# 32 of 384 expert-layer tokens take their input products by gathered rows on GpSimd and ScalarE

## The chip, the cores and the metric

The kernel runs on one core of a Trainium2 chip. The metric is the device time of one execution in microseconds, and the time of a kernel is the median of its runs. The engines are called PE (TensorE, matmuls), DVE (VectorE), ACT (ScalarE), POOL (GpSimd) and SP (SyncE, which only issues DMAs). Times inside an execution are counted from the start of the profiled span.

## The reference, cut to what matters

The program is one transformer layer on 512 tokens of 1024 features: modulated normalisation, a mixer (windowed attention and a gated delta rule), a second normalisation, and then the expert layer. The change is nearly all in the expert layer. It has 16384 experts with one neuron each; every token picks 16 experts in each of 8 heads, so 128 (expert, gate) pairs:

```
def one_block(xt):                                   # 128 tokens x 1024
    q = (xt @ w_query).reshape(PEER_BLOCK, PEER_HEADS, 2, PEER_KEY_HALF)
    s = jnp.einsum('phxd,xkd->phxk', q, sub_keys)    # 128 keys in each half
    s_top, i_top = lax.top_k(s, PEER_TOPK)
    cand = (s_top[:, :, 0, :, None] + s_top[:, :, 1, None, :]).reshape(...)
    best, pos = lax.top_k(cand, PEER_TOPK)
    ...
    expert = i1 * PEER_N_KEYS + i2
    gate = jax.nn.softmax(best, axis=-1)
    act = jax.nn.gelu(jnp.einsum('phkd,pd->phk', u_tab[expert], xt))
    return jnp.einsum('phk,phkd->pd', gate * act, v_tab[expert])
```

The output is sum over the chosen experts of gate times gelu(u_e . x) times v_e. u_tab and v_tab have 16384 rows of 1024 f32 values, 64 MB each.

## The kernel before

The 512 tokens are four tiles of 128, which stand in four *slots*. The SLOT table says which tile stands in which slot.

**Slots 0 to 2 (384 tokens) are dense.** All 16384 experts are computed for them, as 128 groups "e" of 128 experts. For each e, SP loads the 512 KB of the input table (peer_ut) and of the output table (peer_v). ACT and DVE split each load into two f16 parts (t_usplit: ACT L2056, DVE L2058; t_vsplit: ACT L2131, DVE L2133), so that three f16 matmuls stand for one f32 matmul. t_u makes the U product, 24 matmuls of 384 columns per e (8 slices of the features by 3 passes); t_act applies the gelu on ACT and keeps the result (a buffer of `acts`, or a *spill* to DRAM). t_g multiplies it by the gates (DVE L2147), splits it (ACT L2152, DVE L2154), and t_v makes the V product, 18 matmuls of 512 columns per e (3 slots, 2 halves of the features, 3 passes), which add up in six banks over all 128 e. So a V product needs the gates of all 384 tokens, while a U product needs none.

**The gates** are made dense as follows. For each slot the product-key scores are taken (t_q, t_score), and DVE finds the top 16 (t_top, t_slot: MAX8, FIND_INDEX8 and MATCH_REPLACE8 instructions, then a number of small ones; L1925 is the last). Then t_gates makes 8 chunks of 16 tokens per slot: four one-hot instructions of 128x2048 f16 on DVE (L1980, L1982, L1984, L1986), 128 small matmuls that scatter the gates to 128x128 per token, four ACT copies, and a 1 MB write to DRAM (wd). When all 24 chunks are written, the event ev_wall is set, and t_wread, t_vload and t_v start. The wd of eight e at a time is read back in one transfer.

**Slot 3 (128 tokens) is the gather slot.** POOL issues one indirect DMA of 128 rows (512 KB) for each of the 128 choices, first from peer_u, then from peer_v (t_gather, L2224; four row buffers). DVE makes a dot product with each row of peer_u (L2234) and an accumulation with each row of peer_v (L2256).

**The order of instructions.** Every `t_...` function is a task that yields the cost of its next step before issuing it. A planner (Driver) keeps a clock for each engine, and always issues the waiting step of the best priority among those that could start within a small window. Each engine's instruction order in the program is therefore fixed ahead of the run. The dictionary X holds priorities and window sizes. During the run an engine works through its list in that order, and waits where its next instruction isn't ready.

At the program's start ada_group (called by t_ada1) loads the eight 1 MB blocks of the first third of w_ada, and PE multiplies them by the conditioning vector; all else waits for that modulation.

## Time and profile before

| what | value |
|---|---|
| median of 3 runs | 1710.05 us (1708.99 to 1712.87) |
| the profiled execution, its own time | 1712.26 us |
| its span | 1710.5 us |
| PE busy | 1609.8 us, 94% of the span |
| DVE busy | 1444.0 us, 84% |
| ACT busy | 791.0 us, 46% |
| POOL busy | 478.1 us, 28% |
| moved by DMA | 405.16 MB, mean 237 GB/s |
| the chain of work that ended last | PE 39%, DVE 20%, DMA 10% of the span |

Busy shares are means over stages with different limits. The span is best read in three stretches: up to about 635 us the mixer and the queries (the first slot's scoring ends there), from there to about 861 us the scoring and the one-hots, with U products on PE beside them, and from 861 us, where the first V matmul starts, the U and V products with the gathers. The profiled execution's time is 1.8 us over its span.

### The profile page before, as it was taken

How to read it: one execution, taken by the hardware profiler on the slowest of the kernel's cores; microseconds unless marked ns; L12 is line 12 of the kernel's file. 1: busy time of each engine (PE TensorE's matmuls, PEld its weight loads, DVE VectorE, ACT ScalarE, POOL GpSimd, SP SyncE). 2: the span in 40 equal slices, each digit the busy share in tenths (PEclk: the TensorE clock that was granted, in tenths of full speed). 3: DMA queues.
4: the chain of work that ended last, by engine and by line, in shares of the span. 5: the costliest groups of instructions: out<-in, count | busy, mean ns of one | idle time of the engine just before them, and what ended most of it. 6: DMA issues, size and time to landing. Idle time of an engine off the chain costs nothing.

```text
span 1710.5 us, 29276 instructions
## 1 busy us (share of the span) xinstructions
PE 1609.8 (94%) x11075; PEld 978.2 (57%) x11075; DVE 1444.0 (84%) x2884; ACT 791.0 (46%) x1386; POOL 478.1 (28%) x351
## 2 busy tenths in 40 slices
PE   3999998988896999999999999999999999899997
PEld 1665557887655885677655555555555554444443
DVE  3678658988989999999988888888888888798887
ACT  2665658766533434566543333333333333244441
POOL 0200332323001000000014445445466556554300
PEclk9999999999998999999999999999999999999999
DMA  9335442211333303699969999999999999888762
GB/s 378 113 128 187 155 179 81 70 56 45 109 112 134 114 2 124 191 272 279 325 241 354 348 369 344 374 364 350 347 377 330 367 363 331 315 317 331 270 244 86
DMA packets 157727, 405.16 MB, mean 237 GB/s; under 512 B 12681, under 2 KB 71561, under 8 KB 152465
## 3 DMA queue, kind: packets, MB, share of 16 engines
q1 hardware_dynamic: 120720, 269.06, 45.1%
q0 software_dynamic: 36864, 134.23, 21.4%
q8 instruction: 86, 1.41, 0.3%
q14 instruction: 57, 0.46, 0.1%
HBM read 366.59 MB, written 36.65 MB: 236 GB/s over the span
## 4 chain that ended last, share of the span: by engine, by line
PE 39%; DVE 20%; DMA 10%; issue 5%; POOL 2%; ACT 1%; POOLq 0%; DVEq 0%; ACTq 0%; SPq 0%
PE bank L207 38%; DMA arena<-in_peer_v,arena 8%; DVE arena L2058 3%; POOL arena L2224 2%; DVE arena L1986 1%; DVE arena L1984 1%; DVE arena L1980 1%; DVE arena L1982 1%; DVE arena L2256 1%; DMA arena<-in_peer_u,arena 1%; DVE arena L1816 1%; DVE arena L1818 1%; DVE arena L1822 1%; DVE arena L1814 1%; DVE arena L1759 1%
## 5 line engine op out<-in xcount | busy, mean ns | idle before, releaser
L207 PE MATMUL bank<-arena 128*128 128x384 f16 (+9 forms) x10610 | 1566.5, 316 | 49.4 <-DVE arena L1105 6.8
L207 PEld LDWEIGHTS <-arena 128*128 128x128 f16 (+1 forms) x9528 | 826.9, 98 | 626.8 <-issue 46.1
L2224 POOL DMA_INDIRECT arena<-in_peer_u,arena x128 | 161.1, 1258 | 515.2 <-DMA arena<-in_peer_ut 339.0
L2224 POOL DMA_INDIRECT arena<-in_peer_v,arena x128 | 211.8, 1655 | 160.6 <-DVE arena L2256 140.4
L2056 ACT ACTIVATE arena<-arena 128x1024 f16<-128x1024 f32 x128 | 135.1, 1056 | 253.9 <-PE bank L207 184.5
L2131 ACT ACTIVATE arena<-arena 128x1024 f16<-128x1024 f32 x128 | 134.2, 1050 | 136.4 <-PE bank L207 101.0
L2256 DVE SCALAR_TENSOR_TENSOR arena<-arena 128x1024 f32<-128x1024 f32 x126 | 160.2, 1280 | 36.9 <-DMA arena<-in_peer_v,arena 36.7
L2133 DVE TENSOR_TENSOR arena<-arena 128x1024 f16<-128x1024 f32 x128 | 156.0, 1219 | 29.2 <-ACT arena L2131 29.0
L2058 DVE SCALAR_TENSOR_TENSOR arena<-arena 128x1024 f16<-128x1024 f32 x128 | 155.9, 1220 | 26.5 <-ACT arena L2056 26.3
L2234 DVE SCALAR_TENSOR_TENSOR arena<-arena 128x1024 bf16<-128x1024 f32 x128 | 156.3, 1221 | 23.6 <-DMA arena<-in_peer_u,arena 22.8
L2152 ACT ACTIVATE arena<-arena 128x384 f16<-128x384 f32 x128 | 66.4, 519 | 170.6 <-DVE arena L2147 170.4
L207 PEld LDWEIGHTS bank<-arena 128*128 128x128 f32 (+1 forms) x1082 | 114.5, 178 | 36.0 <-DMA arena<-in_w_ada 12.3
L2154 DVE TENSOR_TENSOR arena<-arena 128x384 f16<-128x384 f32 x128 | 70.6, 552 | 6.6 <-ACT arena L2152 6.6
L1063 POOL TENSOR_TENSOR arena<-arena 128x512 f32<-128x512 f32 x12 | 17.9, 1495 | 203.7 <-DVE arena L1060 203.7
L2147 DVE TENSOR_TENSOR arena<-arena 128x384 f32<-128x384 f32 x128 | 70.5, 551 | 1.5 <-DMA arena<-wd 1.5
L1998 ACT ACTIVATE arena<-bank 128x512 f32<-128x512 f32 x96 | 51.7, 598 | 24.9 <-PE bank L207 17.8
L1105 DVE TENSOR_TENSOR arena<-bank,arena 128x512 f16<-128x512 f32 x72 | 49.0, 685 | 15.9 <-PE bank L207 11.5
L2091 ACT ACTIVATE arena<-bank 128x384 f32<-128x384 f32 x128 | 60.7, 475 | 1.6 <-DVE arena L2154 1.2
L1113 ACT ACTIVATE arena<-bank 128x512 f16<-128x512 f32 x60 | 35.8, 597 | 22.4 <-PE bank L207 21.3
L810 DVE SCALAR_TENSOR_TENSOR arena<-arena 128x770 f32<-128x770 f32 (+1 forms) x48 | 44.1, 928 | 0.8
L1529 POOL TENSOR_TENSOR arena<-arena 128x1024 f32<-128x1024 f32 x4 | 9.4, 2348 | 116.5 <-DVE arena L1527 104.0
L1118 ACT ACTIVATE arena<-bank 128x512 f16<-128x512 f32 x60 | 35.5, 596 | 6.2 <-PE bank L207 4.5
(256 smaller groups left out, 1275.0 us busy)
## 6 DMA issues: line engine op xcount, KB each, us to landing
arena<-in_peer_ut SPq DMA_DIRECT2D x128, 512.0 KB, 5.8
arena<-in_peer_v SPq DMA_DIRECT2D x128, 512.0 KB, 6.4
arena<-in_w_ada SPq DMA_DIRECT2D x24, 1024.0 KB, 8.7
wd<-arena SPq DMA_DIRECT2D x24, 1024.0 KB, 6.9
arena<-wd SPq DMA_DIRECT2D x16, 1536.0 KB, 10.3
arena<-in_w_int SPq DMA_DIRECT2D x21, 512.0 KB, 4.4
arena<-in_wq SPq DMA_DIRECT2D x16, 512.0 KB, 3.6
arena<-in_x SPq DMA_DIRECT2D x8, 512.0 KB, 4.6
```

Source lines behind the costliest of these rows:

```text
L207: PE.matmul(out, lhsT=l, rhs=r, start=start, stop=stop, skip_group_check=True)
L2056: A.activation(hl[0], Ud[e], AF.Copy, scale=US)
L2058: V.scalar_tensor_tensor(hl[1], Ud[e], US, hl[0], op0=OP.mult, op1=OP.subtract)
L2091: A.activation(Aw[e], b[:, 0:ND], AF.Gelu, scale=1.0 / US)
L2131: A.activation(hl[0], Vd[e], AF.Copy)
L2133: V.tensor_tensor(hl[1], Vd[e], hl[0], op=OP.subtract)
L2147: V.tensor_tensor(a3, a3, Wr[w][:, :, e % 8], op=OP.mult)
L2152: A.activation(g[0], a, AF.Copy)
L2154: V.tensor_tensor(g[1], a, g[0], op=OP.subtract)
L2224: G.indirect_dma_start(out=r, out_offset=None, in_=io[name], in_offset=bass.IndirectOffsetOnAxis(ap=gidx[:, p:p + 1], axis=0))
L2234: V.scalar_tensor_tensor(scr, r, 1.0, h2g, op0=OP.mult, op1=OP.mult, accum_out=gact[:, p:p + 1])
L2256: V.scalar_tensor_tensor(y, r, gact[:, p:p + 1], y, op0=OP.mult, op1=OP.add)
```

## The change

Thirty-two of the 384 dense tokens, the last 32 of slot 2 (HT = 32, HS = 2), are taken out of the U product, which becomes 352 columns wide (NU). Their activations come from gathered rows, by a new task t_hyb with its helper t_hu: when slot 2's scoring is done, DVE computes the expert numbers (L2240 in the new file), eight DMAs spread them and the 32 tokens' features over 128 partitions (4 choices of a token stand side by side), POOL gathers 32 times 128 rows of peer_u (L2251) into three row buffers, POOL multiplies each by the features (L2259, 128x1024 f32), ACT sums each product along the row (L2261), and at the end come one gelu, four small DMAs back and a DVE product with the gates (L2276). Only then do slot 2's one-hots start (t_gates waits for ev_hyb), and the main gather too. For these 32 columns the dense gate matrix holds gate times activation already, so t_g copies them on ACT rather than multiplying (one more ACT instruction per e), and DVE multiplies 352 columns instead of 384. The V product is as wide as before.

Slot 2, of which the 32 tokens are, is now scored first, then slot 3 and the other two; SLOT puts other tiles in the slots. The three V buffers (vst) are the row buffers of the 32 gathers, handed over after the last of them. ada_group issues its loads before it waits for the conditioning vector. fetch and some other steps tell the planner of extra waiting times ("wait", numbers in X), the limit of spills is 40 instead of 20 (24 are used, before 5), and the numbers in X are other ones.

```diff
-    SLOT = {1: 0, 2: 1, 0: 2, 3: 3}
+    SLOT = {1: 2, 2: 3, 0: 0, 3: 1}
@@ ada_group
         for k in range(KT):
             yield ("spawn", load(k), prio + 0.01 * k)
+        ps = yield get(bank)
+        yield ready
@@ t_ada1
-        b = yield get(pj)
-        yield ev_c0
-        yield from ada_group(0, ada_first, 1, b)
+        b = yield from ada_group(0, ada_first, 1, pj, ev_c0)
@@ _peer
+    HT, HS = 32, 2
+    NU, HQ = ND - HT, 128 // HT
-    vst = Res([reg(101 + 4 * i, [D]) for i in range(3)])
+    vst = Res([])
@@ t_q
+            yield put(hrow, *[reg(kb, [D]) for kb in (57, 61, 65)])
@@ t_gates
+        if s == HS:
+            yield ev_hyb
@@ t_u
-                        mm(b[:, 0:ND], Uw[e][j][:, k], h2hl[i][:, k, 0:ND], k == 0 and n == 0, k == KT - 1 and n == 2)
+                        mm(b[:, 0:NU], Uw[e][j][:, k], h2hl[i][:, k, 0:NU], k == 0 and n == 0, k == KT - 1 and n == 2)
@@ t_g
-            yield dv(ND)
-            V.tensor_tensor(a3, a3, Wr[w][:, :, e % 8], op=OP.mult)
+            yield later(ac(HT, 0, 1))
+            A.activation(a3[:, NCU:], Wr[w][:, NCU:, e % 8], AF.Copy)
+            yield dv(NU)
+            V.tensor_tensor(a3[:, 0:NCU], a3[:, 0:NCU], Wr[w][:, 0:NCU, e % 8], op=OP.mult)
@@ new
+    def t_hyb():
+        yield ev_pair[HS]
+        yield ev_mem1
+        up = slice(128 - HT, 128)
+        i1, i2, g = [pairs[HS]["ii"][up, x].rearrange("p k h -> p (k h)") for x in range(3)]
+        yield dv(128)
+        V.scalar_tensor_tensor(hstage[up], i1, 128.0, i2, op0=OP.mult, op1=OP.add)
+        t = TILE[HS]
+        for q in range(HQ):
+            yield later(dm(HT * 256))
+            sync.dma_start(hidx[q * HT:(q + 1) * HT], hstage[up, q * HT:(q + 1) * HT])
+            yield later(dm(HT * 4096))
+            sync.dma_start(h2g[q * HT:(q + 1) * HT], h2d[(t + 1) * 128 - HT:(t + 1) * 128, :])
+        yield ("join",)
+        for n in range(HT):
+            r = yield get(hrow)
+            yield ("POOL", 1.45)
+            G.indirect_dma_start(out=r, out_offset=None, in_=io["peer_u"],
+                                 in_offset=bass.IndirectOffsetOnAxis(ap=hidx[:, n:n + 1], axis=0))
+            yield ("spawn", t_hu(n, r, g, up), X['pht'])
+    def t_hu(n, r, g, up):
+        yield dm(128 * 4096)
+        yield ("wait", X["whu"])
+        yield ("POOL", 2.9)
+        G.tensor_tensor(r, r, h2g, op=OP.mult)
+        yield ("wait", X["wpa"])
+        yield ac(1100, 0, 1)
+        A.activation(scr, r, AF.Copy, accum_out=hact[:, n:n + 1])
+        yield put(hrow, r)
...
+        yield put(vst, *(yield get(hrow, 3)))
+        yield ac(HT, 0, 1)
+        A.activation(hact, hact, AF.Gelu)
+        for q in range(HQ):
+            yield later(dm(HT * 256))
+            sync.dma_start(hmove[up, q * HT:(q + 1) * HT], hact[q * HT:(q + 1) * HT])
+        yield ("join",)
+        yield ("wait", 5.0)
+        yield dv(128)
+        V.tensor_tensor(g, g, hmove[up], op=OP.mult)
+        yield ("set", ev_hyb)
@@ t_gather
         yield ev_pair[GSLOT]
+        yield ev_hyb
```

The next rows show the start of SP's list, first before, then after (L518 and L521 are the w_ada loads of 1 MB; w_int, w_in, cst and m serve later steps):

```order
L407 DMA arena<-in_w_int 128x1024 x2
L509 DMA arena<-in_b_ada 32x512
L446 DMA arena<-in_cst 128x1280
L509 DMA arena<-in_b_ada 32x512
L631 DMA arena<-in_w_in 128x1152
L448 DMA arena<-in_m 128x1920
L518 DMA arena<-in_w_ada 128x2048 x8
```

```order
L476 DMA arena<-in_ctx 128x1024
L521 DMA arena<-in_w_ada 128x2048
L476 DMA arena<-in_ctx 128x1024
L521 DMA arena<-in_w_ada 128x2048 x2
L409 DMA arena<-in_w_int 128x1024 x2
L449 DMA arena<-in_cst 128x1280
L634 DMA arena<-in_w_in 128x1152
```

The w_ada loads stand ahead of the w_int, cst and w_in loads now, where they stood behind them.

The next rows show POOL's list up to its end, before and after (L1529 is the four products of the second normalisation, which L1532 is after the change; L2224 and L2297 are the gathers of slot 3):

```order
L1314 MEMSET arena 128x8
L1207 TENSOR_TENSOR arena<-arena 128x512
L1314 MEMSET arena 128x8
L1529 TENSOR_TENSOR arena<-arena 128x1024 x4
L2224 DMA arena<-in_peer_u,arena 128x1024 x128
L2224 DMA arena<-in_peer_v,arena 128x1024 x128
```

```order
L2251 DMA arena<-in_peer_u,arena 128x1024 x3
L2259 TENSOR_TENSOR arena<-arena 128x1024 x3
L2251 DMA arena<-in_peer_u,arena 128x1024 x2
L2259 TENSOR_TENSOR arena<-arena 128x1024 x2
L2297 DMA arena<-in_peer_u,arena 128x1024 x128
L2297 DMA arena<-in_peer_v,arena 128x1024 x128
```

Ten rounds of three gathers and three products, and one of two, stand ahead of the first gather of slot 3.

The next rows show DVE's list at the end of the one-hots, before and after (L1986 and L2001 are the fourth one-hot of a chunk, L2058 and L2076 the U split, L1814 to L1841 the scoring of slot 3, L2153 the V split, L2169 the gate product):

```order
L2058 SCALAR_TENSOR_TENSOR arena<-arena 128x1024
L1986 TENSOR_TENSOR arena<-arena 128x2048
L1814 MAX arena<-arena 128x8 x9
L1816 MAX_INDEX arena<-arena 128x8 x9
L1818 MATCH_REPLACE arena<-arena 128x128 x7
L2058 SCALAR_TENSOR_TENSOR arena<-arena 128x1024
```

```order
L1999 TENSOR_TENSOR arena<-arena 128x2048
L2001 TENSOR_TENSOR arena<-arena 128x2048
L2076 SCALAR_TENSOR_TENSOR arena<-arena 128x1024 x5
L2153 TENSOR_TENSOR arena<-arena 128x1024 x2
L2076 SCALAR_TENSOR_TENSOR arena<-arena 128x1024 x2
L2169 TENSOR_TENSOR arena<-arena 128x352
```

The scoring of slot 3, which followed the last one-hot, now stands ahead of it; and between the first slot's scoring and the last one-hot there are 46 U splits instead of 38.

## Rows read from the trace of the kernel before

**Rows 1.** Page, part 1: engine, busy us (share of the span), instructions.
```profile
PE 1609.8 (94%) x11075; PEld 978.2 (57%) x11075; DVE 1444.0 (84%) x2884; ACT 791.0 (46%) x1386; POOL 478.1 (28%) x351
```

**Rows 2.** Windows: the columns are in the first line.
```profile
core 0: us, PE busy (x) PEld busy (x) DVE busy (x) ACT busy (x) POOL busy (x), PEclk, DMA share, GB/s
635.50:832.80 197.30, 193.34 (x1667) 131.76 (x1666) 197.00 (x381) 113.66 (x186) 0.00 (x0) 1.00 0.74 218
800.00:840.00 40.00, 39.19 (x388) 28.40 (x387) 40.00 (x73) 24.84 (x42) 0.00 (x0) 1.00 1.02 301
832.80:890.00 57.20, 53.34 (x317) 29.86 (x317) 51.90 (x200) 25.97 (x37) 0.00 (x0) 0.97 0.82 281
900.00:1000.00 100.00, 100.00 (x558) 54.41 (x556) 84.30 (x123) 37.73 (x52) 49.56 (x39) 1.00 0.95 350
```

**Rows 3.** Groups on PE, 900 to 1400 us: count | busy us, mean ns.
```profile
L207 PE MATMUL bank<-arena 128*128 128x384 f16 x1617 | 269.1, 326 | 0.0
L207 PE MATMUL bank<-arena 128*128 128x512 f16 x1101 | 244.0, 379 | 0.0
```

**Rows 4.** Windows: the first 40 us, columns as in rows 2.
```profile
0.00:20.00 20.00, 0.00 (x0) 0.00 (x0) 14.47 (x46) 6.83 (x8) 0.46 (x10) 1.00 0.92 338
20.00:40.00 20.00, 13.83 (x80) 4.39 (x80) 2.20 (x3) 3.04 (x3) 0.00 (x0) 0.88 1.01 418
```

**Rows 5.** Timeline of PE, one row: start us, us, what [idle before <-releaser].
```profile
40.52 1.87 PE L207 MATMUL bank<-arena 128*32 128x512 f32 x8 [0.61 <-DMA arena<-in_w_ada]
```

**Rows 6.** Lines L1925 and L1986: ns min/median/max, first and last start.
```profile
L1925 DVE TENSOR_TENSOR arena<-arena x4: 267/276/291, 635.5 to 889.7; 128x128 f32<-128x128 f32 x4
L1986 DVE TENSOR_TENSOR arena<-arena x24: 1212/1218/1227, 703.6 to 831.6; 128x2048 f16<-128x2048 f16 x24
```

**Rows 7.** Groups on DVE, 832.8 to 890 us.
```profile
L2058 DVE SCALAR_TENSOR_TENSOR arena<-arena 128x1024 f16<-128x1024 f32 x9 | 11.0, 1217 | 1.2 <-ACT arena L2056 1.1
L2133 DVE TENSOR_TENSOR arena<-arena 128x1024 f16<-128x1024 f32 x5 | 6.1, 1223 | 2.2 <-ACT arena L2131 2.2
L2147 DVE TENSOR_TENSOR arena<-arena 128x384 f32<-128x384 f32 x5 | 2.8, 550 | 1.5 <-DMA arena<-wd 1.5
L2154 DVE TENSOR_TENSOR arena<-arena 128x384 f16<-128x384 f32 x5 | 2.7, 548 | 0.0
```

**Rows 8.** Lines L1529 (GpSimd), L1073 and L392 (VectorE), columns as in rows 6.
```profile
L1529 POOL TENSOR_TENSOR arena<-arena x4: 2338/2351/2354, 505.5 to 549.7; 128x1024 f32<-128x1024 f32 x4
L1073 DVE TENSOR_TENSOR arena<-arena x12: 780/1586/1754, 184.8 to 392.6; 128x512 f16<-128x512 f32 x12
L392 DVE SCALAR_TENSOR_TENSOR arena<-arena x36: 200/219/2382, 471.5 to 1703.8; 128x1 f32<-128x1 f32 x36
```

**Rows 9.** Timeline of GpSimd, one instruction of L1529.
```profile
534.89 2.35 POOL L1529 TENSOR_TENSOR arena<-arena 128x1024 f32<-128x1024 f32 x1 [12.20 <-DVE arena L1527]
```

**Rows 10.** Timeline of VectorE beside L1529's second, third and fourth instruction.
```profile
520.33 2.38 DVE L392 SCALAR_TENSOR_TENSOR arena<-arena 128x1 f32<-128x1 f32 x1
535.35 2.97 DVE L1759 SCALAR_TENSOR_TENSOR arena<-arena 128x1024 f16<-128x1024 f32 x1 [0.54 <-ACT arena L1757]
550.15 0.28 DVE L1820 MAX8 arena<-arena 128x8 f32<-128x128 f32 x1
```

**Rows 11.** Chain of waits: start us, us, what.
```profile
836.61 7.05 DMA wd<-arena
850.83 0.56 DVE arena L2147
861.00 1.09 PE bank L207 x3
```

**Rows 12.** Line L2224, the gathers: columns as in rows 6.
```profile
L2224 POOL DMA_INDIRECT arena<-in_peer_u,arena x128: 932/1014/1991, 891.1 to 1226.7; - x128
L2224 POOL DMA_INDIRECT arena<-in_peer_v,arena x128: 932/1309/4416, 1229.0 to 1598.2; - x128
DMA to landing us min/median/max: 4.3/7.3/12.1
```

More of the change, by code (lines that the diff above doesn't have):

```diff
@@ L113, in _advance @@
                 t.ready = max(t.ready, t.join)
+            elif s[0] == "wait":
+                t.ready = max(t.ready, t.join) + s[1]
             elif s[0] == "spawn":
@@ L527, in ada_group @@
             yield put(ring, ws[k])
+        return ps
     def t_ada1():
@@ L1987, in chunk @@
             yield ("join",)
+            yield ("wait", X["ww"])
             wb = yield get(wbs)
@@ L2003, in chunk @@
             sync.dma_start(wd[:, :, s * 8 + n].rearrange("w p i t -> p w i t"), wb.rearrange("p (w i) t -> p w i t", i=8))
+            yield ("wait", X["ws"])
             yield put(wbs, wb)
@@ L2128, in t_vsplit @@
             yield evVd[e]
+            if e == 0:
+                yield ev_wall
+                yield put(acts, *actr(101, 8))
             hl = yield get(vhl)
@@ L2222, in t_gather @@
                 r = yield get(grow)
-                yield pl(450)
+                yield ("POOL", 1.45)
                 G.indirect_dma_start(out=r, out_offset=None, in_=io[name],
@@ L2232, in t_gu @@
         yield dm(128 * 4096)
+        yield ("wait", X["wg"])
         yield dv(1024, 1)
@@ L2247, in t_gv @@
         yield dm(128 * 4096)
+        yield ("wait", X["wg"])
         yield ev_ga
```

69 lines of the change are left out of this document (41 added, 28 removed).

## The prediction

> **What bounds the kernel now.** I read the engine totals first, then the windows, since the totals mix stages. PE is busy 94% of the span and DVE 84% [rows 1]. By stage [rows 2], the stretch from the first slot's scoring to the last one-hot (635.5 to 832.8 us) has DVE busy 197.0 of 197.3 us, and PE 193.3: both are full there, but only DVE's work leads to ev_wall, so DVE sets when the V products may start. Towards its end the DMA engines are full too (share 1.02, though only 301 GB/s, from 800 to 840). The 57 us after the last one-hot hold 51.9 us of DVE work. From 900 us on PE is busy 100 of 100 us and DVE 84, with DMA at 0.95: here PE sets the pace. So the time is a sum of two parts with different limits: the start of V, by DVE, and what PE has to do from there on.
>
> **The change: U products of 352 columns.** Between 900 and 1400 us a matmul of 384 columns takes 269.1/1617 = 166.4 ns of PE's time and one of 512 columns 244.0/1101 = 221.6 ns [rows 3], which is 0.431 ns for a column. (The means that the rows print, 326 and 379 ns, overlap one another.) 32 columns are 13.8 ns, a matmul of 352 is 152.6 ns, and 128 x 24 = 3072 matmuls save 42.4 us in all. But only what is saved behind the start of V counts in the end, and the rest is idle time for PE ahead of it.
>
> **The start.** PE's last wait for a w_ada load ends at 40.5 us [rows 5], and from 20 to 40 us 418 GB/s were moved [rows 4]. The loads of w_int, cst, w_in and m that stood ahead of it are 2.7 MB (two of 512 KB, then 640, 576 and 480 KB), which is 6.7 us at that rate. They now arrive last instead, by about 41 us, and are needed after the modulation. I take -6 us, with the bounds 0 (the next step then waits for w_int) and -7.
>
> **DVE's stretch ahead of the last one-hot.** Before, it runs from the first L1925 at 635.5 to the last L1986 at 831.6 + 1.2 = 832.8 us [rows 6]. What stands ahead of the first L1925 is the same in both orders. Inside, the new order has two additions. First the scoring of slot 3: of the 51.9 us after 832.8, the U splits are 11.0, the V splits 6.1, the gate products 2.8 and 2.7 [rows 7], and one last piece of a gate product about 1.2; the remaining 28.1 us are that scoring. Second, 8 more U splits by 1.22 us (11.0/9), 9.8 us. Sum 37.9 us; without any cost of GpSimd the last one-hot would end at 635.5 - 6 + 197.3 + 37.9 = 864.7. L2240, L2276 and the split conversions are small instructions and together under 1 us.
>
> **What GpSimd's products cost DVE.** POOL did nothing in that stretch [rows 2]; now it makes 32 products of 128x1024 f32 there. The same form takes 2.35 us [rows 8]. What DVE does beside one is seen at three places. One of L1529 began at 534.89 [rows 9]; the DVE instruction with two inputs in SBUF that began at 535.35 took 2.97 us [rows 10], where its form takes 1.22 [rows 7]: 1.75 lost. Beside another, L392 took 2.38 us where its median is 0.22 [rows 8, 10]: 2.16 lost. Beside the last, a MAX8, with one input, took its normal 0.28 [rows 10]. L1073, two inputs again and beside GpSimd products of its own stage, has a median of 1.59 us and a minimum of 0.78 [rows 8]. So a two-input instruction waits until the GpSimd product ends, and a one-input instruction doesn't. Between L2240 and L2276 DVE's list holds 37 U splits and 59 one-hots and 12 other products of 128x2048, 108 instructions of two inputs at 1.22 us, 132 us; the whole piece is 197.3 + 37.9 = 235.2 less the 9 splits and 37 one-hots that follow L2276 (46 x 1.22 = 56.1), 179 us. That is 74%, and with the small products of the scoring about 80%. I take 0.8 x 32 x 2.0 = **51 us**; the bounds are 0 (nothing is lost on f16 one-hots, and the splits happen to lie elsewhere) and 32 x 2.35 = 75.
>
> The Trainium skill, page "SBUF — State Buffer", section "Who interferes with whom", says of this that a VectorE instruction with two SBUF inputs contends with a GpSimd instruction that reads SBUF for a pair of ports under an exclusive lock, and that the one issued second is blocked fully. For the f32 rows above the trace agrees (1.75 and 2.16 of 2.35 us); that it holds for one-hots of f16, which are most of the stretch, no row here shows, and by that rule the loss is the 51 us above rather than nothing.
>
> **Does DVE wait for the 32 rows themselves?** L2276 stands 179 + 51 = 230 us behind L2240 on DVE, with 37 one-hots and 9 U splits, and so ev_wall, queued behind it. The chain to it: index and spreading DMAs about 10 us; 10.7 rounds of three gathers. A round is one issue of 1.0 us, a landing of 7.3 [rows 12], three products of 2.35, and about 2 us in which the products wait for DVE instructions under way: 17.5 us, 187 in all; then sum, gelu, four DMAs, 8 us. That makes 205 us, 25 less than DVE needs. With landings of 12.1 us, the slowest of the gather's two phases [rows 12], it is 10.7 x 22.3 + 18 = 257, and DVE would wait 27. I take nothing, and keep 27 for the range.
>
> **From the last one-hot to the first V matmul.** Before, the last wd write began at 836.6, the first gate product at 850.8 and V at 861.0 [rows 11], 28.2 us behind the last one-hot. Of these the first 18.0 (copies, write, reading back) stay. The other 10 were DVE finishing the first V splits behind slot 3's scoring; now two V splits stand ahead of the first gate product, so 3.5 us remain (product, copy, split). Together 21.5. V then starts at 864.7 + 51 + 21.5 = 937.2, 76 us later than before.
>
> **From there to the end.** Before, 84 U products were left at 861.0 (44 stood ahead in PE's order): 84 x 24 x 166.4 ns + 2304 x 221.6 ns = 335.5 + 510.6 = 846.1, against 849.5 measured. In the new order 54 stand ahead: 74 x 24 x 152.6 ns + 510.6 = 781.6, and with the same 3.4 on top 785 us. DVE's 84% [rows 2] are work of the same size less the slot 3 scoring, so it doesn't take over. The extra ACT copy in each e stands on an engine busy 38%. The 24 spills and reloads instead of 5 are 19 x 2 x 180 KB, 7 MB, 20 us of one stretch's 350 GB/s spread over 1000 us. The gathers of slot 3 took 1598.2 - 891.1 = 707 us before [rows 12]; 30 us behind the start of V plus 707 plus 15 is 752, less than 785.
>
> **The sum:** 937.2 + 785 = 1722.2 us of span. The profiled execution before had 1712.3 with a span of 1710.5, and the median of the runs is 1710.05, 0.45 under that span. So I forecast **1722 us**, 0.7% slower: 64.5 us less PE work behind the start of V, and a start that is 76 us later. It breaks even where GpSimd's products cost 39 us, 1.23 us each.
>
> **Rivals.**
>
> (a) *The products cost DVE little or nothing.* For it: no row shows a 128x2048 f16 instruction beside a GpSimd product; GpSimd may be the one that waits, as its list has 25 us of slack. Against it: three forms that all lost, one of them of almost no work. With nothing lost V starts at 886.2 and the end is 1671; if the splits alone are hit (45 of 179 us, 0.25 x 64 = 16 us) 1687. Where DVE is no longer the limit, DMA may be: at a share of 1.02 [rows 2] the wd writes, U loads and 32 gathers (16.8 MB, 56 us at 301 GB/s, half of it hidden) take up to 28 us back, 1699. So 1671 to 1706, faster. Chance 0.33.
>
> (b) *The chain of 32 rows is the end of the stretch.* Slow landings while wd writes and U loads fill the DMA engines: 27 us as worked out, 1749. It decides once a round takes over (230 - 18)/10.7 = 19.8 us. Chance 0.11.
>
> (c) *The gathers of slot 3 end last.* From 752 us behind V they reach 785 if one takes 2.90 us instead of 2.77 (707/255); the loads that PE now consumes 4% faster are what could slow them. At 3.05 it is 30 + 778 + 15 = 823, and the end 1760. Against it: the order of bytes is nearly unchanged, and the last 112 us before held no gather. Chance 0.08.
>
> **How the numbers follow.** The forecast's own case (a loss of 1.2 to 2.35 us for each product) has 0.48 and reaches from 1709 to 1746; a measurement can tell some 0.2%, 3.4 us, from no change, so its lowest part, 0.08, is "same". Faster by more than that is nearly all of (a), 0.31, with 0.02 of it in "same"; with a little of the remaining ends "same" is 0.11. Slower is the remaining 0.40 of the forecast, with (b) and (c), 0.58 in sum. The range is 1680 to 1755: (a) at its cleanest, below 1680, and (c) are left out, about 0.1 each. The likeliest case alone would be 1709 to 1746.
>
> **What would show it.** In the changed kernel's trace: the first 40 us shorter by some 6; U matmuls of 153 ns; U splits and one-hots beside L2259 that take 2.5 to 3.5 us instead of 1.22, some 26 of 32 products hitting one; the last one-hot near 916 us and V near 937; PE idle some 50 to 100 us between 640 and 937; PE full from there. It is wrong if one-hots keep 1.22 us beside L2259 (then (a)), if DVE sits idle ahead of L2276 (then (b)), or if PE waits for loads or the last gather behind 1650 us (then (c)).

## The result and the profile after

The changed kernel takes 1785.96 us (1784.59 to 1787.68) against 1711.22 us for the kernel before, measured together: a ratio of 1.0437, interval 1.042 to 1.0453. The forecast was 1722 us with a range up to 1755. The direction was right and the size was not: 75 us slower instead of 11. The profiled execution's span is 1784.8 us, 62.6 us over the 1722.2 of the sum.

The engine totals of the changed kernel's page, which answer to [rows 1]:

```profile
PE 1607.2 (90%) x11075; PEld 987.7 (55%) x11075; DVE 1499.9 (84%) x2887; ACT 837.0 (47%) x1579; POOL 603.3 (34%) x415
```

PE's busy time fell by 2.6 us only, although 42.4 us of columns are gone. Its mean granted clock fell with it, from 0.984 to 0.958 (busy time multiplied by that clock, an estimate since the clock is a mean over the whole span, is 1584 before and 1540 after, which has the 42 us in it). Where that happened is seen in the windows of the changed kernel (columns as in rows 2): first scoring to last one-hot, from there to the first V product, and the last stage in three pieces.

```profile
639.70:951.20 311.50, 234.71 (x1846) 160.95 (x1845) 298.32 (x567) 158.70 (x272) 144.58 (x64) 0.87 0.71 219
951.20:982.80 31.60, 28.63 (x232) 19.80 (x230) 11.30 (x11) 15.98 (x27) 3.79 (x4) 1.00 1.00 327
982.80:1400.00 417.20, 417.19 (x2128) 207.76 (x2129) 355.21 (x531) 173.33 (x299) 173.35 (x132) 1.00 0.97 359
1400.00:1720.00 320.00, 312.25 (x1746) 168.79 (x1745) 279.63 (x288) 127.47 (x210) 171.72 (x119) 1.00 0.95 352
1720.00:1784.80 64.80, 44.74 (x204) 20.13 (x202) 52.08 (x107) 16.74 (x26) 1.67 (x1) 0.80 0.37 130
```

The first stretch, 197.3 us in [rows 2], now lasts 311.5, and PE is busy in 235 of it at a mean granted clock of 0.87: it stops and goes. In the second, DVE works 11 of 32 us and PE 29: there PE is what is late, not DVE. The chain of waits, which answers to [rows 11], says the same (start us, us, what):

```profile
897.55 1.23 DVE arena L2001
898.77 0.14 DVE arena L1977
898.91 0.04 issue
898.96 64.78 PE bank L209 x618
...
966.17 6.13 DMA wd<-arena
...
972.38 8.60 DMA arena<-wd
...
981.62 0.54 DVE arena L2169
...
982.81 17.22 PE bank L209 x73
```

From 899 to 964 us the chain is 618 matmuls in a row: it is not the last one-hot, at 951, that ends late, but PE's list behind a one-hot of 897. V starts at 982.8, 122 us later than before and 45.6 later than predicted; from there to the end it takes 802.0 us instead of the predicted 785, another 17.0.

**The blocked instructions** are there as described. The products of GpSimd, one pair of them in its timeline, and VectorE beside it:

```profile
L2259 POOL TENSOR_TENSOR arena<-arena x32: 2337/2484/3352, 652.9 to 863.1; 128x1024 f32<-128x1024 f32 x32
```

```profile
860.46 5.97 POOL L2259 TENSOR_TENSOR arena<-arena 128x1024 f32<-128x1024 f32 x2 [2.52 <-DMA arena<-in_peer_u,arena]
```

```profile
859.72 1.21 DVE L1999 TENSOR_TENSOR arena<-arena 128x2048 f16<-128x2048 f16 x1
860.86 3.37 DVE L2076 SCALAR_TENSOR_TENSOR arena<-arena 128x1024 f16<-128x1024 f32 x1
864.15 3.37 DVE L2001 TENSOR_TENSOR arena<-arena 128x2048 f16<-128x2048 f16 x1
```

A split and an f16 one-hot take 3.37 us instead of 1.22 beside a product, 2.15 lost in each, and the two products of 2.35 us take 5.97 together: the engines take turns there. They don't always. One VectorE instruction that began at 672.56 us took 6.08 us, its form's longest, and waited out three products in a row; a conversion that began at 658.81 us took 2.43:

```profile
671.59 6.96 POOL L2259 TENSOR_TENSOR arena<-arena 128x1024 f32<-128x1024 f32 x3
L1883 DVE TENSOR_SCALAR arena<-arena x20: 211/218/6081, 623.9 to 855.6; 128x128 uint32<-128x128 uint32 x20
L1852 DVE CAST arena<-arena x4: 365/376/2433, 615.7 to 798.5; 128x256 f16<-128x256 uint32 x4
```

Both have one input. So the prediction's reading that a one-input instruction doesn't wait, taken from one MAX8, holds for the instructions of the top-16 search (none took over 0.3 us more than its median beside a product) and not for these two.

From 639.7 to 951.2 us, 25 DVE instructions or groups took over 0.3 us more than the median of their form, 57 us in sum, 7.9 of it on those two; GpSimd's 32 products took 86.5 us by the page's groups instead of 32 x 2.35 = 75.

### The profile page after: what moved, and what is told of

It reads as the page before. It is cut to its first block, busy times and chain, and to the rows that moved or that the text cites. A ratio compares the mean times of both kernels' runs of the same rounds, so it can differ in the third digit from the quotient of the medians.

```text
span 1784.8 us, 29695 instructions
## 1 busy us (share of the span) xinstructions
PE 1607.2 (90%) x11075; PEld 987.7 (55%) x11075; DVE 1499.9 (84%) x2887; ACT 837.0 (47%) x1579; POOL 603.3 (34%) x415
## 4 chain that ended last, share of the span: by engine, by line
PE 37%; DVE 20%; DMA 11%; issue 6%; POOL 3%; ACT 1%; DVEq 0%; POOLq 0%; SPq 0%; ACTq 0%
PE bank L209 36%; DMA arena<-in_peer_v,arena 8%; DVE arena L2076 4%; DVE arena L2331 2%; DMA arena<-in_peer_u,arena 1%; POOL arena L2251 1%; DVE arena L2001 1%; POOL arena L2297 1%; DVE arena L1999 1%; DVE arena L1995 1%; DVE arena L1997 1%; DMA arena<-wd 0%; DVE arena L1883 0%; DVE arena L1921 0%; DVE arena L1923 0%
## 5 line engine op out<-in xcount | busy, mean ns | idle before, releaser
L209 PE MATMUL bank<-arena 128*128 128x352 f16 (+8 forms) x10610 | 1564.6, 317 | 143.8 <-DVE arena L2076 52.0
L209 PEld LDWEIGHTS <-arena 128*128 128x128 f16 (+1 forms) x9528 | 837.5, 100 | 689.1 <-DVE arena L2076 66.2
L2297 POOL DMA_INDIRECT arena<-in_peer_u,arena x128 | 165.2, 1290 | 344.2 <-DVE arena L2308 224.6
L2297 POOL DMA_INDIRECT arena<-in_peer_v,arena x128 | 185.4, 1448 | 160.7 <-DVE arena L2331 140.2
L2153 DVE TENSOR_TENSOR arena<-arena 128x1024 f16<-128x1024 f32 x128 | 156.4, 1223 | 55.4 <-ACT arena L2151 55.3
L2074 ACT ACTIVATE arena<-arena 128x1024 f16<-128x1024 f32 x128 | 134.9, 1054 | 144.8 <-PE bank L209 138.0
L2076 DVE SCALAR_TENSOR_TENSOR arena<-arena 128x1024 f16<-128x1024 f32 x128 | 173.2, 1353 | 32.8 <-ACT arena L2074 32.4
L2308 DVE SCALAR_TENSOR_TENSOR arena<-arena 128x1024 bf16<-128x1024 f32 x128 | 156.2, 1220 | 12.2 <-DMA arena<-in_peer_u,arena 11.7
L2175 ACT ACTIVATE arena<-arena 128x384 f16<-128x384 f32 x128 | 66.8, 522 | 202.9 <-DVE arena L2169 202.6
L2251 POOL DMA_INDIRECT arena<-in_peer_u,arena x32 | 58.1, 1816 | 159.1 <-DVE arena L1827 101.6
L2259 POOL TENSOR_TENSOR arena<-arena 128x1024 f32<-128x1024 f32 x32 | 86.5, 2724 | 16.8 <-DMA arena<-in_peer_u,arena 16.7
L2169 DVE TENSOR_TENSOR arena<-arena 128x352 f32<-128x352 f32 x128 | 66.3, 518 | 3.9 <-DMA arena<-wd 3.9
L2109 ACT ACTIVATE arena<-bank 128x352 f32<-128x352 f32 x128 | 57.4, 448 | 4.7 <-PE bank L209 4.2
L1532 POOL TENSOR_TENSOR arena<-arena 128x1024 f32<-128x1024 f32 x4 | 12.4, 3093 | 103.3 <-DVE arena L1530 103.3
L1116 ACT ACTIVATE arena<-bank 128x512 f16<-128x512 f32 x60 | 35.8, 597 | 20.0 <-PE bank L209 17.8
```

Of the source, the lines that this page charges most:

```text
L209: PE.matmul(out, lhsT=l, rhs=r, start=start, stop=stop, skip_group_check=True)
L2074: A.activation(hl[0], Ud[e], AF.Copy, scale=US)
L2076: V.scalar_tensor_tensor(hl[1], Ud[e], US, hl[0], op0=OP.mult, op1=OP.subtract)
L2153: V.tensor_tensor(hl[1], Vd[e], hl[0], op=OP.subtract)
L2175: A.activation(g[0], a, AF.Copy)
L2251: G.indirect_dma_start(out=r, out_offset=None, in_=io["peer_u"], in_offset=bass.IndirectOffsetOnAxis(ap=hidx[:, n:n + 1], axis=0))
```

## The experiments

All times are medians; the kernel before, run beside them, had medians of 1712 to 1714 us. The table has, from each profile, the end of the last one-hot (its last start plus 1.2), the first V product and the span. (In the kernels that keep the old order a single V matmul began up to 2.6 us sooner, and the next one waited for the second V split; the table has the start of the row of V matmuls, as the 861.0 of before is.)

| kernel | last one-hot | first V | span | median |
|---|---|---|---|---|
| before | 832.8 | 861.0 | 1710.5 | 1711 |
| predicted | 915.7 | 937.2 | 1722.2 | 1722 |
| after | 951.2 | 982.8 | 1784.8 | 1786 |
| e1, no products | 900.7 | 933.1 | 1736.1 | 1733 |
| e2, no rows at all | 883.2 | 914.5 | 1711.7 | 1717 |
| e15, gathers alone | 883.6 | 915.5 | 1715.0 | 1715 |
| e3, dots on VectorE | 922.4 | 954.6 | 1750.0 | 1751 |
| e14, e2 with fewer U ahead | 870.8 | 892.3 | 1735.9 | 1742 |
| e6, before with 352 columns | 833.1 | 861.4 | 1696.6 | 1699 |
| e9, before, fewer gathers | 833.1 | 861.0 | 1698.4 | 1702 |
| e10, e6, fewer gathers | 833.7 | 863.1 | 1678.2 | 1681 |
| e11, after, fewer gathers | 952.3 | 984.3 | 1777.0 | 1777 |
| e13, before with products | 881.8 | 911.1 | 1755.6 | 1758 |
| e12, before with earlier products | 846.9 | 875.0 | 1720.8 | 1724 |
| e4, before, new ada_group | 850.4 | 875.6 | 1726.9 | 1730 |
| e5, after, planner told | 982.7 | 1013.2 | 1809.7 | 1805 |
| e7, after, old ada_group | 952.8 | 984.9 | 1788.7 | 1787 |
| e8, after, late scoring | 940.7 | 989.8 | 1794.2 | 1793 |

**The products and the rows: e1, e2, e3.** In e1 GpSimd's product is left out, in e2 the gathers too (ScalarE sums the features), both in the changed kernel's instruction order:

```diff
-        G.tensor_tensor(r, r, h2g, op=OP.mult)
```
```diff
-            G.indirect_dma_start(out=r, ..., in_=io["peer_u"], ...)
-        G.tensor_tensor(r, r, h2g, op=OP.mult)
-        A.activation(scr, r, AF.Copy, accum_out=hact[:, n:n + 1])
+        A.activation(scr, h2g, AF.Copy, accum_out=hact[:, n:n + 1])
```

> The changed kernel in the same instruction order, with GpSimd's 32 products left out (ScalarE sums the raw gathered rows, so the activations of the 32 tokens are not the reference's). Theory 1, the products block VectorE and what is late after that counts too (VectorE lost 57 us to them in the trace, waited 12 us for ScalarE and TensorE, and the first V product came 10 us later behind the last one-hot than I had worked out): all of it goes, 1785 - 79 = about 1705. Theory 2, only the blocked time itself goes: 1785 - 57 = 1728. Theory 3, the chain of gathers, landings and sums ends last anyway: 1755 or more. No one-hot or U split over 1.3 us under any of them.

> As e1_no_product, and the 32 gathers are left out too (ScalarE sums the tokens' features instead, so again other activations). Under theories 1 and 2 the gathers cost nothing beside the products: within 5 us of e1_no_product. Under theory 3 the gathers and landings are the end of the stretch: 30 us or more under e1_no_product. What is left against the kernel before is then the 352-column U product, the start and the new plan: 1671 was worked out for that in the prediction.

e1 took 1733 us, so the products are worth 53 us, nearest to the 57 of theory 2; V starts 49.7 us sooner, and 51 was predicted. No one-hot took over 1.23 us:

```profile
L2001 DVE TENSOR_TENSOR arena<-arena x24: 1218/1224/1231, 733.4 to 899.5; 128x2048 f16<-128x2048 f16 x24
```

But e2 took 1717, another 16 us less (18.6 at the first V product) for gathers that I had put at nothing (at most 5 us under theories 1 and 2). And with no rows at all the new kernel is no faster than the kernel before (1.0023, interval 1.0004 to 1.0042), where I had worked out 1671. So the larger error is not in the products at all.

In e3 the dots are on VectorE:

```diff
-        yield ("POOL", 2.9)
-        G.tensor_tensor(r, r, h2g, op=OP.mult)
-        yield ("wait", X["wpa"])
-        yield ac(1100, 0, 1)
-        A.activation(scr, r, AF.Copy, accum_out=hact[:, n:n + 1])
+        yield ("wait", 5.0)
+        yield dv(1024, 1)
+        V.scalar_tensor_tensor(scr, r, 1.0, h2g, op0=OP.mult, op1=OP.mult, accum_out=hact[:, n:n + 1])
```

> The changed kernel with the 32 products and sums on VectorE, one fused instruction each (as the gather slot has them, 1.28 us and a readout of 0.08), and none on GpSimd or ScalarE; the planner sees that. Theory 1: VectorE pays 32 x 1.36 = 44 us instead of 57 lost, and the plan holds, so the 22 us behind it go as well: 1785 - 13 - 22 = about 1750. Theory 2: 1785 - 13 = 1772. Theory 3: VectorE stands in its list ahead of each late row, 1785 or more.

1751 us, as theory 1 had it, though not by its reasons: V starts 40.1 us behind e2's, close to the dots' own time there (39.1 us, and 2.8 for their readouts). The planner laid out the engines anew for e3, so this comparison is less clean than that of e1 with e2. One instruction on the bounding engine is cheaper than a product on an engine that blocks it and a sum on a third (68 us behind e2). It is the fastest of the kernels that have the change's whole work, and still 2.2% slower than before.

**What the gathers cost: e15.** ScalarE's sum is L2262 in the changed kernel ("The change" has L2261) and L2261 in e1, which has one line less. In e1 ScalarE waits for a late row at the head of its list; behind it there stand the copy out of PE's bank (L2109) and the next split (L2074), for which VectorE waits in turn. GpSimd, ScalarE and VectorE in e1:

```profile
804.98 17.33 POOL L2251 DMA_INDIRECT arena<-in_peer_u,arena  x1 [7.45 <-ACT arena L2261]
```

```profile
825.61 1.06 ACT L2261 ACTIVATE arena<-arena 128x1024 bf16<-128x1024 f32 x1 [9.71 <-DMA arena<-in_peer_u,arena]
826.57 0.19 ACT L2261 ACTIVATION_READ_ACCUMULATOR arena<-arena 128x1 f32 x1
826.78 1.28 ACT L2109 ACT_TABLE_LOAD   x1
828.07 0.46 ACT L2109 ACTIVATE arena<-bank 128x352 f32<-128x352 f32 x1
828.43 1.05 ACT L2074 ACTIVATE arena<-arena 128x1024 f16<-128x1024 f32 x1
```

```profile
829.51 1.22 DVE L2076 SCALAR_TENSOR_TENSOR arena<-arena 128x1024 f16<-128x1024 f32 x1 [6.76 <-ACT arena L2074]
```

e15 has the 32 gathers, but nothing on ScalarE waits for their rows:

```diff
-        G.tensor_tensor(r, r, h2g, op=OP.mult)
-        A.activation(scr, r, AF.Copy, accum_out=hact[:, n:n + 1])
+        A.activation(scr, h2g, AF.Copy, accum_out=hact[:, n:n + 1])
```

> The changed kernel with its 32 gathers but no products, and ScalarE summing the tokens' features instead of the rows, so that nothing in ScalarE's list waits for a row (other activations, again). If ScalarE's in-order wait for late rows makes the 19 us between e1_no_product and e2_no_rows: as e2_no_rows, 1709 to 1717. If the gathers' traffic or their issue does: as e1_no_product, 1728 to 1736.

1715 us, with V at 915.5: as e2. So the 18.6 us come by way of ScalarE's in-order wait; the traffic and the issue of the gathers cost nothing by themselves, not even one issue of 36 us.

What made the rows late in e1 stands in its trace. ScalarE waited for a row at two places only, 17.0 us in all, each behind a gather whose issue on GpSimd had lasted 19.75 or 17.33 us instead of about 1. The second is shown above; the first, and the VectorE split behind it:

```profile
703.00 19.75 POOL L2251 DMA_INDIRECT arena<-in_peer_u,arena  x1 [6.47 <-ACT arena L2261]
728.16 1.23 DVE L2076 SCALAR_TENSOR_TENSOR arena<-arena 128x1024 f16<-128x1024 f32 x1 [6.22 <-ACT arena L2074]
```

These two waits of VectorE, 6.22 and 6.76 us, are 13 of the 15.5 us by which it is idle for longer in e1's stretch (20.0 us) than in e2's (4.5). The changed kernel itself has one such issue, 17.43 us long, and VectorE is idle for 13.2 us, 8.7 more than in e2. There the 68 us between its last one-hot and e2's are nearly all accounted for by 57 of blocked instructions, 8.7 of idle time and 1.7 of a later first scoring. So the products cost more and the rows less than the differences between e1, e2 and the changed kernel say, since without products the rows held VectorE up for longer.

**The price of a product by itself: e12 and e13.** Both add products to the kernel before, on a free buffer, with the other engines' orders unchanged:

```diff
+        G.memset(r, 1.0)
+        for n in range(32):
+            G.tensor_tensor(r, r, r, op=OP.mult)
```

> The kernel before, in its own order, with 32 GpSimd products of 128x1024 f32 on a free buffer added behind the first slot's scoring, back to back, and nothing else (the result is unchanged). The price of the products as predicted, 2.0 to 2.2 us of VectorE each where its instructions have two inputs: 51 to 70 us, so 1762 to 1780. If the price in the changed kernel came of its chain of gathers rather than of VectorE: under 1730.

1724 us, 11 us more. Nothing in e12 held the products back until the first scoring was done, and they ran beside the top-16 search from 555 us on, where most of VectorE's instructions have one input:

```profile
L2213 POOL TENSOR_TENSOR arena<-arena x32: 1892/1893/2755, 555.2 to 624.1; 128x1024 f32<-128x1024 f32 x32
```

So it measured something else than it was made for: 0.34 us for a product beside that search (0.44 by the start of V). e13 makes the first product read the transposed gates of slot 0:

```diff
+        G.memset(r, 1.0)
+        p = lockT[0][:, :, 0]
+        G.tensor_tensor(r[:, 0:128], p, p, op=OP.subtract)
+        for n in range(32):
+            G.tensor_tensor(r, r, r, op=OP.mult)
```

> The kernel before, in its own order on all other engines, with 32 GpSimd products of 128x1024 f32 that start with the first one-hots (they wait for data of that step), back to back; the result is unchanged. They took 1.9 us each in e12_before_products, where VectorE ran mostly one-input instructions and lost 11 us in all. Beside one-hots and splits, all with two inputs: if VectorE waits each of them out, 32 x 1.7 to 1.9 = 54 to 61 us, and as the end moves with the start of V, 1767 to 1774. If GpSimd is the one that waits, or f16 one-hots are not hit: 1713 to 1725.

1758 us: 45 us more, below the expected 54 to 61. The products ran from 643 us, beside splits and the rest of the scoring, with the one-hots yet to come:

```profile
L2219 POOL TENSOR_TENSOR arena<-arena x32: 1893/2020/3168, 642.9 to 714.5; 128x1024 f32<-128x1024 f32 x32
```

```profile
L1989 DVE TENSOR_TENSOR arena<-arena x24: 1205/1215/1227, 752.6 to 880.6; 128x2048 f16<-128x2048 f16 x24
```

The last one-hot ends 49 us later than before, 1.53 us for a product of 1.9 to 2.0, and the end is 45 later. So a price near the predicted 1.6 us (51/32) comes out without gathers and without a new plan, and the end moves with the start of V. The one-hots kept their 1.22 us in e13, behind the last product; that they are hit too, the changed kernel's timeline alone shows.

**What the columns are worth: e6, e9, e10, e11.** e6 is the kernel before with the U product at 352 columns and no work in their place:

```diff
-                        mm(b[:, 0:ND], Uw[e][j][:, k], h2hl[i][:, k, 0:ND], ...)
+                        mm(b[:, 0:NU], Uw[e][j][:, k], h2hl[i][:, k, 0:NU], ...)
-            V.tensor_tensor(a3, a3, Wr[w][:, :, e % 8], op=OP.mult)
+            A.activation(a3[:, NCU:], Wr[w][:, NCU:, e % 8], AF.Copy)
+            V.tensor_tensor(a3[:, 0:NCU], a3[:, 0:NCU], Wr[w][:, 0:NCU, e % 8], op=OP.mult)
```

> The kernel before in its own instruction order, with the U product 352 columns wide and the 32 columns' gates copied by ScalarE as after the change; nothing takes the place of the 32 tokens' activations, so that part of the result is left out. Theory A, TensorE sets the pace from the first V product on, and ahead of it VectorE does: the 84 U products behind it save 84 x 24 x 13.8 ns = 28 us, 1711 - 28 = 1683. Theory B, transfers and the gathers of slot 3 set the pace there (the DMA share is 0.95 to 0.97 for 700 us): most of the 28 us become waits, 1700 or more.

1699 us, 14 us less, half of the 28. A column is worth what was predicted (between 1000 and 1400 us a matmul of 352 took 191.5/1248 = 153 ns in e6), but PE, which waited for nothing from 1000 to 1400 us before, now waits. From the first V product to the end PE's busy time fell by 24 us (829.2 to 805.4), and its idle time rose by 10 (20.3 to 29.9). The window of before and that of e6:

```profile
1000.00:1400.00 400.00, 400.00 (x2162) 211.33 (x2160) 344.49 (x443) 150.62 (x207) 206.85 (x151) 1.00 0.96 360
```

```profile
1000.00:1400.00 400.00, 394.34 (x2202) 215.30 (x2201) 351.52 (x453) 157.46 (x263) 203.09 (x153) 1.00 0.97 368
```

PE's waits of e6 between 640 us and the end (in all, times, longest), for V splits (L2135), gate splits (L2155) and U splits (L2060), where before had 5.5, 5.5 and 1.7 us:

```profile
PE bank L207 <- DVE arena L2135: 9.0, 7, 2.6
PE bank L207 <- ACT arena L2155: 8.3, 7, 3.2
PE bank L207 <- DVE arena L2060: 7.6, 13, 1.7
```

e9, e10 and e11 leave out every second gather of peer_v, in before, e6 and after:

```diff
+                if name == "peer_u" or p % 2 == 0:
                     G.indirect_dma_start(...)
```

> The kernel before with every second gather of peer_v left out (64 of 256 gathers, 34 MB; VectorE still accumulates, on rows left in the buffers, so slot 3's result is wrong). If TensorE alone sets the pace of the last stage: no change, 1711 to 1713. If gathers, landings and the accumulations that VectorE's list holds ahead of the splits set part of it: 3 to 15 us less.

> e6_before_352 with the same 64 gathers left out. If transfers took the other half of the saved columns (e6_before_352 got 14 us of 28): 1683 to 1687, 12 to 16 us less than e6_before_352 and 26 to 30 less than e9_before_half. If the columns aren't worth 13.8 ns each, or something else takes them: 14 us less than e9_before_half, as it was without it.

> The changed kernel with the same 64 gathers left out. Its last stage, from the first V product to the end, took 802 us where 785 were predicted from TensorE's work. If transfers make the difference: 785 to 790 of that stage, 1768 to 1773 in all. If TensorE does (waits at the tail, a lower clock): 800, and 1783 to 1787.

e9 1702, e10 1681, e11 1777. With fewer gathers the columns are worth 21 us instead of 14 (20.2 by the spans), between the two expectations; 34 MB of gathers are worth 12 us to the kernel before, 18 to e6 and 9 to the changed kernel. From the first V product on e10 takes 815 us, 3 under the 818 that the times of PE's matmuls give (84 x 24 x 152.6 ns + 510.6), and e9's 837 is 9 under its 846. PE's idle time in that stage falls from 20.3 to 11.2 us in e9 and from 29.9 to 15.6 in e10: in both old-order kernels the gathers, landings and accumulations take their share of the last stage beside PE, and more of it in e6, where PE has less to do.

**What makes V late behind the last one-hot: e8 and e14.** e8 holds the scoring of slot 3 back until the gates are written:

```diff
         row, v, i = sc, stop[s][:, hx], itop[s][:, hx]
+        if s == GSLOT:
+            yield ev_wall
```

> The changed kernel with the scoring of slot 3 held back until the last gates are written, where it stood before the change. If VectorE sets the start of V: its stretch is 32 us shorter, and V starts that much sooner, while VectorE has room for the scoring behind it: 1755 to 1760. If TensorE does, with the 54 U products that stand ahead of V now: 1780 to 1790, since fewer U products ahead only move behind.

1793 us. The last one-hot ended 10 us sooner (940.7), and the first gate product not at all (984.4 against 981.6). So an earlier last one-hot alone doesn't bring V forward. Which list V waits for e8 doesn't show: it was planned anew, 58 U products stand ahead of V instead of 54, and VectorE works on the held-back scoring right up to that gate product. e14 is e2 with NSPILL at 10 instead of 40:

```diff
-    NSPILL = 40
+    NSPILL = 10
```

> e2_no_rows with at most 10 spilled U products instead of 24, so some 14 fewer U products and U splits ahead of V, and none between the last one-hot and the first V split in VectorE's list (7 before). If those splits, which wait for TensorE, make V late: the first V product 18 to 22 us behind the last one-hot instead of 31, and near 890 us instead of 914; the 14 products then run behind it and cost 14 x 3.7 = 51 us there, so the end is not earlier, 1710 to 1740. If something else does: 31 us again, and V near 905.

V starts 21.5 us behind the last one-hot, where it was 31.3, and the chain of waits goes from the last one-hot through 8 matmuls and the copies to the wd write:

```profile
869.61 1.24 DVE arena L2001
870.89 0.62 PE bank L209 x8
873.67 10.91 DMA wd<-arena
```

In e2 it goes, as in the changed kernel, through 618 matmuls in a row (64.9 us from 830.9 on), which start 52 us ahead of the end of the last one-hot. So the U products in PE's list are what took the 10 us. The seven U splits between the last one-hot and the first gate product show it on VectorE: they wait for ScalarE's part, and that for PE to free a buffer, as the timeline of the changed kernel has it:

```profile
949.96 1.22 DVE L2001 TENSOR_TENSOR arena<-arena 128x2048 f16<-128x2048 f16 x1
951.11 1.22 DVE L2076 SCALAR_TENSOR_TENSOR arena<-arena 128x1024 f16<-128x1024 f32 x1
955.01 1.23 DVE L2076 SCALAR_TENSOR_TENSOR arena<-arena 128x1024 f16<-128x1024 f32 x1 [2.69 <-ACT arena L2074]
960.38 1.23 DVE L2076 SCALAR_TENSOR_TENSOR arena<-arena 128x1024 f16<-128x1024 f32 x1 [4.14 <-ACT arena L2074]
964.85 1.23 DVE L2076 SCALAR_TENSOR_TENSOR arena<-arena 128x1024 f16<-128x1024 f32 x1 [3.25 <-ACT arena L2074]
```

The whole is 24 us slower for it (1742), since the U products come behind V instead.

**The start and the plan: e4, e5, e7.** e4 is the kernel before with the new ada_group and its two callers alone, e7 the changed kernel with the old ones:

```diff
         for k in range(KT):
             yield ("spawn", load(k), prio + 0.01 * k)
+        ps = yield get(bank)
+        yield ready
```

That is e4's edit, and e7's is the reverse. e5 is the changed kernel with a step that tells the planner of 1.8 us of VectorE for each product:

```diff
+        yield ("DVE", 1.8, "a")
         yield ("POOL", 2.9)
         G.tensor_tensor(r, r, h2g, op=OP.mult)
```

> The kernel before with the change of ada_group alone (w_ada loads ahead of the w_int, cst and w_in loads). If the 7 us that the modulation comes earlier are kept to the end: 1704. If the mixer's other loads and engines absorb it, as the changed kernel's trace suggests (its first scoring ends 4 us later than before, not 6 earlier): 1708 to 1712.

> The changed kernel with ada_group as before (w_ada loads behind w_int, cst and w_in), planned anew. The kernel before got 17 us slower by the new ada_group alone. If the early loads themselves cost that: 1785 - 17 = 1768. If it was the plan that came out of it, and the changed kernel's numbers are fitted to theirs: 1785 or more.

> The changed kernel, with the planner told that each product of GpSimd takes 1.8 us of VectorE's time (no instruction is added; the order of all engines is planned anew). If the waits behind the blocked time (12 us of VectorE for splits ahead of the last one-hot, some 12 us more than planned from there to the first gate product) come of a plan that doesn't know of it: 1785 - 24 = about 1761. If they are TensorE's own load: 1780 to 1790.

e4 took 1730, 17 us more than the kernel before, outside both expectations; e7 1787, no difference, so in the changed kernel the loads' order is worth nothing; e5 1805, outside both again. Any change of a task makes the planner lay out the engines anew. In e5, which adds no instruction and no transfer, that alone moves the end by 19 us. For e4's 17 us it is the likely cause but not shown, since the loads' order changed with it: the modulation comes 7 us sooner (35.5 against 42.5 us) and the first scoring ends 17 us later (653.0 against 635.5). So e3, e4, e5, e7 and e8 tell less than the runs that keep the order (e1, e2, e6, e9 to e13, e15); e14's order differs from e2's by the limit of spills.

## Why the prediction was right in direction and wrong in size

Five steps failed. The two largest are that the chain of the 32 rows costs VectorE nothing (18.6) and that PE alone sets the pace of the last stage (17.0); the others are the length of DVE's stretch (10.0), the way from the last one-hot to V (9.8) and the start (8.5). By the prediction's own steps, in us of the profiled executions:

- **The products' cost to VectorE: right in kind and size, with some luck.** 51 predicted, 49.7 between e1 and after at the first V product, 57 blocked in the changed kernel's own trace, and 49 in e13 without any of the rest. That f16 one-hots are hit like f32 splits, which no row of before showed, is in the timeline above. The Trainium skill ("SBUF — State Buffer", section "Who interferes with whom") says of any VectorE instruction with two SBUF inputs that it contends with a GpSimd instruction that reads SBUF, and the trace agrees: 3.37 us instead of 1.22. A discount for one-input instructions was needed as well (0.34 us for a product in e12), but not for all of them: 7.9 of the 57 us fell on two instructions of one input, which the working had left out.
- **"I take nothing" for the chain of 32 rows: wrong, 18.6.** I looked for the wait at L2276 alone. L2276 did not wait: VectorE had no idle time ahead of it. But the 32 sums stand in ScalarE's list between copies and splits, and those behind a late row wait with it (e15). The step named what is queued behind DVE's waiting instruction, and left out what is queued behind ScalarE's. It also counted 1.0 us for every issue of a gather; the late rows are those behind issues of 17 to 20 us. In the changed kernel, with one such issue, the rows cost 8.7 us of VectorE's time and not 18.6.
- **The last one-hot to V, 21.5: wrong by 10.** The working was right for a list with two V splits there, and e14 gives 21.5. The list has seven U splits as well, which stood in the order rows ahead of the prediction, and I priced them at nothing. VectorE had time for them; PE, which had the U products to make, had not: it worked without a pause from 899 to 964 us.
- **-6 us at the start: wrong by 10 (by 8.5 in e2, whose first scoring ends at 638.0; the sum below uses that).** The modulation does come 7.0 us sooner:

```profile
36.25 1.06 PE L209 MATMUL bank<-arena 128*128 128x8 f32 x8 [0.82 <-DVE arena L541]
```

  (it started at 43.2 before), but the first scoring ends at 639.7, 4.2 later than in [rows 6]. At the first GpSimd product of the second normalisation 2.5 of the 7 us are left (503.0 against 505.5), and e7, with the old loads, has its first scoring at 641.5: the gain is used up on the way, in engines whose order is another one too; which instruction loses it is open. I had taken it that nothing before the first scoring changes, from the list of instructions; the list was the same in number and not in order.
- **DVE's stretch, without the rows: wrong by 10.** 235.2 predicted, 245.2 in e2. Some three of them are idle time, most of it for ScalarE's splits. The other 7 I can't assign to one line; part is that the added scoring and conversions take more than the 28.1 us that the window behind the last one-hot had shown.
- **The last stage, 785: 802, wrong by 17.** Its premise was that PE alone sets the pace there, from a window with PE busy 100 of 100 us. That was true of the window and not of the whole stage: the two groups of [rows 3] overlap and add up to 513 us in 500, so the times of a matmul were 2.6% too high, which hid that PE was idle for 20.3 of the 849.5 us. e6 shows that half of what is saved there is lost. The stage of before, that of the changed kernel, and two pieces of the changed kernel's end:

```profile
861.00:1710.50 849.50, 829.23 (x4318) 423.06 (x4317) 715.77 (x966) 317.22 (x429) 372.89 (x256) 0.99 0.87 321
982.80:1784.80 802.00, 774.17 (x4074) 396.69 (x4074) 686.91 (x924) 317.54 (x534) 346.74 (x252) 0.98 0.91 338
1734.00:1746.00 12.00, 5.78 (x12) 0.93 (x12) 10.36 (x15) 7.89 (x15) 0.00 (x0) 0.54 0.64 219
1746.00:1760.00 14.00, 13.95 (x51) 5.72 (x52) 11.06 (x27) 3.06 (x3) 0.00 (x0) 0.78 0.19 73
```

  With the old 20.3 us of idle time the 785 leave PE busy for 764.7; it was busy for 774.2, 9.5 more, and idle for 27.8, 7.5 more. e11 gives 9 of the 17 back with fewer gathers, and with them go the waits for U splits (L2076), 6.8 us from 1400 us on. Some 6 more are at the end: the last U product ends at 1732.5, and from 1734 to 1760 us 63 V matmuls take 19.7 us, with waits for gate splits (L2175) between them and granted clocks of 0.54 and 0.78, where 14.0 would do at 222 ns each. Before, the U products ended at 1486, and in the last 65 us PE was busy for 54 at a clock of 0.95, without a wait up to its last matmul. The remaining 2 us are open.

The sum: 8.5 + 10.0 + 9.8 (e2 against the 886.2 predicted without product costs) - 1.3 + 18.6 + 17.0 = 62.6.

Of the rivals, (b) was right that the chain of rows costs something and wrong on where; (c), the gathers at the end, has a part in the 17 us. (a) had it that without the products' cost the time would be 1671. It is 1712 to 1717 (e2): the whole of the change, with its 32 rows for nothing, gains nothing. That is the largest miss in all, 28.3 us ahead of V and 12.2 behind it: of the 42 us of columns I let 25 count in the last stage at once (74 of the 128 U products), and I took the ten U products moved ahead of V (40 us at 384 columns) as free, since PE was to be idle there. PE was idle there, for 77 us in the changed kernel's first stretch, but not where those products needed it: its list and VectorE's wait for each other by turns, and from 899 us on there are 65 us in which only PE is behind.

No version among these beats the kernel before with its whole work done. e3 is the nearest; its dots cost 40 us, and the columns are worth 14 in the old plan.

## What to carry to other kernels

An engine that is busy 100% in a window is the bound for the work it has now; before counting what less work saves, look how far behind it the next limit is (here a DMA share of 0.96 and splits in the lists of two engines), and don't count all of the saving (here half of it was lost). Work put on an "idle" engine costs what it blocks and what stands behind its results in every in-order list: for each added wait, go through the lists of all engines that read the result, not only the last one. And where a planner lays out all engines anew, the same kernel with an edit that adds no instruction can move by 1% (e5), so an experiment should keep the order and leave out instructions.

## What the runs showed of the hardware that was not expected

The issue of a gather on GpSimd, in the changed kernel 0.93 to 2.1 us for 31 of the 32 of peer_u that the change adds, now and then lasted until about the time of a pause of VectorE. In the changed kernel one took 17.43 us, and ended 0.8 us after VectorE had run out of work (its idle time of 6.58 us before 751.02 began at 744.44):

```profile
727.82 17.43 POOL L2251 DMA_INDIRECT arena<-in_peer_u,arena  x1 [1.39 <-ACT arena L2262]
```

```profile
743.76 0.68 DVE L1926 TENSOR_TENSOR arena<-arena 128x1024 f16<-128x1024 f16 x1
751.02 3.53 DVE L2076 SCALAR_TENSOR_TENSOR arena<-arena 128x1024 f16<-128x1024 f32 x1 [6.58 <-ACT arena L2074]
```

The same came in e1 (19.75 us, and 17.33 us, the second ending 0.45 us before VectorE's last instruction did), in e7, e8 and e11 (16.6 to 17.4 us), and in e15:

```profile
701.12 36.32 POOL L2251 DMA_INDIRECT arena<-in_peer_u,arena  x1 [2.33 <-DMA arena<-in_peer_u,arena]
```

There it lasted 36.32 us, and ended 0.8 us after the start of a pause of VectorE of 0.74 us. VectorE's instructions took no longer by it; what it lost was the wait for the late row, where its next split hung on that row (6.58 us here, 6.22 and 6.76 in e1, nothing in e15). No experiment was made on it: that a pause ends the issue is read from six of these seven cases, and which of VectorE's instructions would hold it up is open, since most issues beside the same one-hots took 1 to 2 us.
